# Transposes, casts and differences of a gated block over both token halves in one instruction

## The chip, the cores and the metric

The kernel runs on one core of a Trainium2 chip. The metric is the device time of one execution in microseconds; the time given for a kernel is the median of its runs. Engines are named as the profile does: PE is TensorE (PEld its weight loads), DVE is VectorE, ACT is ScalarE, POOL is GpSimd, SP is SyncE.

## The reference

One decoder block over 256 tokens of width 2048, in float32. A feed-forward block (FFN), a mixer, a second FFN and a gated embedding each add to `h`:

```python
def swiglu(x, w_gu, w_down):
    gate, up = jnp.split(x @ w_gu, 2, axis=-1)
    return (jax.nn.silu(gate) * up) @ w_down

h = h + 0.5 * swiglu(rms_norm(h, ffn1_norm[i]), ffn1_w_gu[i], ffn1_w_down[i])
h = h + hybrid_mixer(rms_norm(h, mix_norm[i]), w_in[i], ...)
h = h + 0.5 * swiglu(rms_norm(h, ffn2_norm[i]), ffn2_w_gu[i], ffn2_w_down[i])
gate = jax.nn.sigmoid(rms_norm(h, ple_norm[i]) @ ple_w_gate[i])
h = h + gate * (p[i] @ ple_w_proj[i])
```

The hidden width of an FFN is 5632. The change lies in the two FFNs alone, between `silu(gate) * up` and the product with `w_down`.

## The kernel before

**Products.** Every float32 operand of a large product is split into a rounded half `hi`, of type fp32r, and the remainder `lo`; a product is then three matmuls, hi by hi, hi by lo and lo by hi (lines L540, L541 and L542 in the FFNs). The stationary operand is a 128x128 piece of the activations, transposed (features on the partitions, tokens along the row), and the moving one is 128x512 of weights. The split of weights is done as they arrive: ACT casts (`whi`, L74) and DVE subtracts (`wlo`, L75), on tiles of 128x1024. Part of the FFNs' products goes by a scheme with seven products instead of eight on half matrices; it needs sums of weights (`R`, L304 and L311), which are split by L295 (ACT, `shi`) and L296 (DVE, `slo`), their matmuls are L334 to L336, and L341 and L342 add intermediate results.

**An FFN.** The hidden width is 11 blocks of 512, in three parts of 3, 4 and 4 blocks (`PARTS`). For each block the gate and up products of both token halves (t = 0 and 1, 128 tokens each) end in PSUM; after a part's blocks come that part's products with `w_down`, in two groups of 1024 output columns. The last block of a part is therefore needed soonest after it is made.

**The block of the change**, `down_input`, once per block, 22 times in the kernel. For both token halves: L477 multiplies up and silu(gate) into `sil` (128 tokens by 512 features per half). L482 transposes 32x32 squares of it on DVE into `tb`, one instruction per half. The squares are then brought into place by DMAs through DRAM: L487 writes `tb` to `scr`, L491 and L492 read it back into `tT`, in four pieces. L499 casts `tT` on ACT to `hTh`, the hi half, and L500 subtracts on DVE to `hTl`; again one instruction per token half. `hTh` and `hTl` are the stationary operands of the down products, 4 pieces of 128 features by 256 tokens per tile. The DMAs are issued on ACT's queue, and on SP's for the last block of a part.

**Order.** `down_input` is a generator that is advanced once per step of the weight stream, so its parts stand in the program between other work: after the transposes, and eight steps (for the last block of a part, two or three) before the casts. Two instructions that depend on one another wait by semaphores; each engine runs its own queue in order. A planner sets the order of each queue when the program is built, from its own estimate of when each instruction's inputs are ready, with the program's order as the priority. `keep` in the code, for all but the last block of a part, holds an instruction at its place in the program's order.

The same chain of transposes is also in `transposed` (L169) for the norms and the mixer, and a like split in `gate` (L1273); they stay as they are.

Of the kernel before, what the change touches and what calls it, by code (L numbers as in the profile page):

```python
# [13 lines left out]
ALU = mybir.AluOpType  # L14
AX = mybir.AxisListType

P = 128
# [26 lines left out]
def block_kernel(ctx, tc, a, out):  # L44
    nc = tc.nc
# [418 lines left out]
    def ffn(n, nT, r, scale, next_norm, stat):  # L464
        xs = picker(*nT)
        late = callable(r)
        with tc.tile_pool(name="ffn", bufs=1) as fp:
            hTh, hTl = [], []

            def down_input(u, sil, th, tl, last):  # L470

                queue, keep = (nc.sync, lambda x: x) if last else (nc.scalar, tc.keep_in_program_order)
                for t in range(2):
                    nc.vector.scalar_tensor_tensor(out=sil[:, t, :], in0=u[t], scalar=r[:, t:t + 1], in1=sil[:, t, :],  # L477
                                                   op0=ALU.mult, op1=ALU.mult)
                yield
                tb = fp.tile([P, 4, 2, P], F32, tag="tT", name="tb")  # L480
                for t in range(2):
                    nc.vector.transpose(tb[:, :, t].rearrange("p c (j x) -> p c j x", j=4),  # L482
                                        sil[:, t, :].rearrange("p (j c x) -> p c j x", j=4, c=4))
                if not last:
                    yield
                scr = dr.tile([P, 4, 2, P], F32, tag="scr2", name="scr2", bufs=2)
                keep(queue.dma_start(out=scr, in_=tb))  # L487
                for _ in range(2):
                    yield
                tT = fp.tile([P, 4, 2, P], F32, tag="tT", name="tT")  # L490
                for c in range(4):  # L491
                    keep(queue.dma_start(out=tT[32 * c:32 * c + 32].rearrange("x q t i -> x q (t i)"),  # L492
                                         in_=scr[:, c].rearrange("(q x) t i -> x q (t i)", q=4)))
                for _ in range(last or 8):
                    yield
                for t in range(2):
                    hi, lo = (x[:, :, t * P:(t + 1) * P].rearrange("p j (q y) -> p q j y", q=4) for x in (th, tl))
                    tv = tT[:, :, t].rearrange("p q (j y) -> p q j y", j=4)
                    keep(nc.scalar.copy(hi, tv))  # L499
                    keep(nc.vector.tensor_tensor(out=lo, in0=tv, in1=hi, op=ALU.subtract))  # L500

            def gated(g):
                sil = fp.tile([P, 2, NB], F32, tag="sil", name="sil")
                for t in range(2):
                    nc.scalar.activation(sil[:, t, :], g[t], AF.Silu, scale=r[:, t:t + 1])
                return sil
# [4 lines left out]
            for group, todo in ffn_plan[n]:  # L511
# [15 lines left out]
                for kind, one in todo:  # L527
# [5 lines left out]
                    for j in range(2):  # L533
# [3 lines left out]
                        for t in range(2):  # L537
                            c = slice(t * P, (t + 1) * P)
                            out = group.banks[2 * b + t]
# [19 lines left out]
                    elif b == 0:  # L559
                        if not late:  # L560
                            sil = gated(outs)
                    else:
                        if late:
                            r = r()
                            sil = gated(group.banks[0:2])
                            late = False
                        th = fp.tile([P, 4, T], F32R, tag="hTh", name="hTh", bufs=max(i1 - i0 for i0, i1 in PARTS))
                        tl = fp.tile([P, 4, T], F32R, tag="hTl", name="hTl", bufs=max(i1 - i0 for i0, i1 in PARTS))
                        hTh.append(th)
                        hTl.append(tl)  # L570
                        i0, i1 = PARTS[group.part]

                        last = (3 if i1 - i0 == 4 else 2) if len(hTh) == i1 else 0
                        gen = down_input(outs, sil, th, tl, last)
                        next(gen)

                        lanes.finish(0)
                        lanes.add(0, gen)
                        if last:
                            lanes.advance(0)  # L580
# [58 lines left out]
    with tc.tile_pool(name="fin", bufs=1) as fp:  # L639
# [35 lines left out]
        for _, (nb, g) in todo:  # L675
            whi, wlo = next_weights()
            for j in range(2):
                k = 2 * g + j
                xh, xl = xs(k)
                for t in range(2):  # L680
                    c = slice(t * P, (t + 1) * P)
# [17 lines left out]
        for t in range(2):  # L699
# [6 lines left out]
            for j in range(4):  # L706
                c = slice(j * NB, (j + 1) * NB)
# [670 lines left out]
```

## Time and profile before

| what | value |
|---|---|
| median of 3 runs | 1947.38 us (1946.30 to 1947.69) |
| span of the profiled execution, first to last instruction | 1944.1 us |
| median less that span | 3.3 us |
| PE busy / DVE busy / ACT busy | 1927.9 / 1603.2 / 1163.4 us |
| mean granted TensorE clock | 0.999 |
| L482 transposes | 44, 30.3 us in all |
| L499 casts | 44, 25.0 us in all |
| L500 differences | 44, 28.7 us in all |

The profile gives of the profiled execution its span, from the first to the last instruction; a time of its own beyond that isn't recorded. Busy shares are averages over stages. An instruction's duration and the time until the next one of its engine starts are two things, as the next can start before the first has ended.

### The profile page before, as it was taken

How to read it: one execution, taken by the hardware profiler on the slowest of the kernel's cores; microseconds unless marked ns; L12 is line 12 of the kernel's file. 1: busy time of each engine (PE TensorE's matmuls, PEld its weight loads, DVE VectorE, ACT ScalarE, POOL GpSimd, SP SyncE). 2: the span in 40 equal slices, each digit the busy share in tenths (PEclk: the TensorE clock that was granted, in tenths of full speed). 3: DMA queues.
4: the chain of work that ended last, by engine and by line, in shares of the span. 5: the costliest groups of instructions: out<-in, count | busy, mean ns of one | idle time of the engine just before them, and what ended most of it. 6: DMA issues, size and time to landing. Idle time of an engine off the chain costs nothing.

```text
span 1944.1 us, 24295 instructions
## 1 busy us (share of the span) xinstructions
PE 1927.9 (99%) x8882; PEld 1593.1 (82%) x8882; DVE 1603.2 (82%) x1743; ACT 1163.4 (60%) x1358; POOL 148.8 (8%) x226
## 2 busy tenths in 40 slices
PE   9999999999999999999999999999999999999998
PEld 7888888888888888878788888888888888888887
DVE  7879988998889866797856679899888998889965
ACT  6655656566665567654555456566565755657654
POOL 0010110000001000010100000011000100001000
PEclk9999999999999999999999999999999999999999
DMA  8778898898898765556464776788898988989864
GB/s 306 269 217 291 256 292 272 248 296 247 269 288 255 224 218 171 173 167 218 159 215 157 243 278 229 236 268 285 260 278 253 306 257 261 264 263 273 253 212 147
DMA packets 144183, 475.06 MB, mean 244 GB/s; under 512 B 19648, under 2 KB 47296, under 8 KB 129856
## 3 DMA queue, kind: packets, MB, share of 16 engines
q1 hardware_dynamic: 104896, 293.78, 43.6%
q0 software_dynamic: 25920, 160.44, 29.9%
q10 hardware_dynamic: 13248, 19.30, 3.3%
q8 instruction: 69, 1.13, 0.2%
q14 instruction: 50, 0.41, 0.1%
HBM read 451.44 MB, written 22.02 MB: 244 GB/s over the span
## 4 chain that ended last, share of the span: by engine, by line
PE 91%; DVE 6%; issue 1%; DMA 1%; ACT 1%; POOL 0%; SPq 0%; POOLq 0%; DVEq 0%; ACTq 0%
PE d L540 5%; PE d L541 5%; PE d L542 5%; PE u L541 5%; PE u L542 5%; PE u L540 5%; PE g L541 4%; PE g L542 4%; PE pj L109 4%; PE pj L110 4%; PE pj L111 4%; PE g L540 4%; PE g L335 4%; PE g L334 4%; PE g L336 4%; PE u L334 3%
## 5 line engine op out<-in xcount | busy, mean ns | idle before, releaser
L74 ACT CAST whi<-raw 128x1024 fp32r<-128x1024 f32 (+1 forms) x489 | 511.7, 1050 | 420.0 <-PE pj L111 108.9
L75 DVE TENSOR_TENSOR wlo<-raw,whi 128x1024 fp32r<-128x1024 f32 (+1 forms) x489 | 590.8, 1217 | 155.8 <-ACT whi L74 153.1
L296 DVE TENSOR_TENSOR slo<-R,shi 128x2048 fp32r<-128x2048 f32 (+2 forms) x224 | 444.4, 1987 | 99.9 <-ACT shi L295 99.7
L295 ACT CAST shi<-R 128x2048 fp32r<-128x2048 f32 (+2 forms) x224 | 374.0, 1673 | 185.6 <-DVE R L304 74.4
L109 PE MATMUL pj<-whi,nTh 128*128 128x512 f32 x448 | 179.4, 401 | 0.0
L110 PE MATMUL pj<-wlo,nTh 128*128 128x512 f32 x448 | 175.3, 391 | 1.4 <-DVE wlo L75 1.4
L111 PE MATMUL pj<-whi,nTl 128*128 128x512 f32 x448 | 174.9, 390 | 0.0
L541 PE MATMUL d<-wlo,hTh 128*128 128x512 f32 x448 | 174.4, 389 | 0.0
L542 PE MATMUL d<-whi,hTl 128*128 128x512 f32 x448 | 174.0, 389 | 0.0
L540 PE MATMUL d<-whi,hTh 128*128 128x512 f32 x448 | 173.1, 390 | 0.0
L541 PE MATMUL g<-wlo,nTh 128*128 128x512 f32 x400 | 156.1, 390 | 0.6 <-DVE wlo L75 0.6
L540 PE MATMUL g<-whi,nTh 128*128 128x512 f32 x400 | 154.9, 390 | 1.2 <-ACT whi L74 0.9
L542 PE MATMUL g<-whi,nTl 128*128 128x512 f32 x400 | 155.9, 390 | 0.0
L541 PE MATMUL u<-wlo,nTh 128*128 128x512 f32 x400 | 155.7, 389 | 0.1
L542 PE MATMUL u<-whi,nTl 128*128 128x512 f32 x400 | 155.6, 389 | 0.0
L540 PE MATMUL u<-whi,nTh 128*128 128x512 f32 x400 | 154.2, 389 | 0.0
L304 DVE TENSOR_TENSOR R<-R 128x2048 f32<-128x2048 f32 (+2 forms) x68 | 135.4, 1991 | 0.1
L110 PEld LDWEIGHTS pj<-wlo,nTh 128*128 128x128 f32 x448 | 84.2, 188 | 19.2 <-DVE wlo L75 3.0
L540 PEld LDWEIGHTS d<-whi,hTh 128*128 128x128 f32 x448 | 84.1, 188 | 17.9 <-ACT hTh L499 0.7
L542 PEld LDWEIGHTS d<-whi,hTl 128*128 128x128 f32 x448 | 84.1, 188 | 17.7
L111 PEld LDWEIGHTS pj<-whi,nTl 128*128 128x128 f32 x448 | 84.1, 188 | 17.5
L541 PEld LDWEIGHTS d<-wlo,hTh 128*128 128x128 f32 x448 | 84.1, 188 | 17.4
(327 smaller groups left out, 3482.5 us busy)
## 6 DMA issues: line engine op xcount, KB each, us to landing
raw<-in_w_gu SPq DMA_DIRECT2D x199, 512.0 KB, 5.7
raw<-in_w_down SPq DMA_DIRECT2D x112, 512.0 KB, 6.4
raw<-in_w_in SPq DMA_DIRECT2D x112, 512.0 KB, 3.4
R<-in_w_gu2q POOLq DMA_DIRECT2D x54, 1024.0 KB, 8.1
R<-in_w_gu1q POOLq DMA_DIRECT2D x48, 1024.0 KB, 8.7
raw<-in_w_out SPq DMA_DIRECT2D x32, 512.0 KB, 4.4
R<-in_w_down11q POOLq DMA_DIRECT2D x12, 768.0 KB, 6.8
R<-in_w_down12q POOLq DMA_DIRECT2D x12, 768.0 KB, 6.3
```

What stands on the lines that cost most here:

```text
L74: nc.scalar.copy(hi[:, j, :], raw[:, j, :])
L75: nc.vector.tensor_tensor(out=lo[:, j, :], in0=raw[:, j, :], in1=hi[:, j, :], op=ALU.subtract)
L109: nc.tensor.matmul(outs[t], xh[:, c], whi[:, j, :], start=st, stop=False)
L110: nc.tensor.matmul(outs[t], xh[:, c], wlo[:, j, :], start=False, stop=False)
L111: nc.tensor.matmul(outs[t], xl[:, c], whi[:, j, :], start=False, stop=sp)
L295: keep(nc.scalar.copy(hi, w))
L296: nc.vector.tensor_tensor(out=lo, in0=w, in1=hi, op=ALU.subtract)
L304: keep(nc.vector.tensor_tensor(out=self.raw[x], in0=self.raw[x], in1=self.raw[y], op=ALU.add))
L334: nc.tensor.matmul(out, xh, whi[:, g, :], start=st, stop=False, skip_group_check=True)
L540: nc.tensor.matmul(out, xh[:, c], whi[:, j, :], start=st, stop=False, skip_group_check=True)
L541: nc.tensor.matmul(out, xh[:, c], wlo[:, j, :], start=False, stop=False, skip_group_check=True)
L542: nc.tensor.matmul(out, xl[:, c], whi[:, j, :], start=False, stop=sp, skip_group_check=True)
```

## The change

In `down_input`, the loops over t around L482 and around L499 and L500 are gone. The transposes of both halves are one instruction on a view with one more dimension, and so are the cast and the difference. What is computed, the tiles and the DMAs stay. Each of the three kinds goes from 44 instructions of 128x512 to 22 of 128x1024; `hTh` and `hTl` are each written by one instruction for both token halves.

```diff
                 tb = fp.tile([P, 4, 2, P], F32, tag="tT", name="tb")
-                for t in range(2):
-                    nc.vector.transpose(tb[:, :, t].rearrange("p c (j x) -> p c j x", j=4),
-                                        sil[:, t, :].rearrange("p (j c x) -> p c j x", j=4, c=4))
+                nc.vector.transpose(tb.rearrange("p c t (j x) -> p c t j x", j=4),
+                                    sil.rearrange("p t (j c x) -> p c t j x", j=4, c=4))
                 if not last:
                     yield
...
                 for _ in range(last or 8):
                     yield
-                for t in range(2):
-                    hi, lo = (x[:, :, t * P:(t + 1) * P].rearrange("p j (q y) -> p q j y", q=4) for x in (th, tl))
-                    tv = tT[:, :, t].rearrange("p q (j y) -> p q j y", j=4)
-                    keep(nc.scalar.copy(hi, tv))
-                    keep(nc.vector.tensor_tensor(out=lo, in0=tv, in1=hi, op=ALU.subtract))
+                hi, lo = (x.rearrange("p j (t q y) -> p t q j y", t=2, q=4) for x in (th, tl))
+                tv = tT.rearrange("p q t (j y) -> p t q j y", j=4)
+                keep(nc.scalar.copy(hi, tv))
+                keep(nc.vector.tensor_tensor(out=lo, in0=tv, in1=hi, op=ALU.subtract))
```

## The prediction

> **What bounds the kernel now.** I read the page's busy times first, then who TensorE waited for, then three stretches of time, then the instructions around the changed lines.
>
> ```profile
> span 1944.1 us, 24295 instructions
> PE 1927.9 (99%) x8882; PEld 1593.1 (82%) x8882; DVE 1603.2 (82%) x1743; ACT 1163.4 (60%) x1358; POOL 148.8 (8%) x226
> PEclk9999999999999999999999999999999999999999
> PE 91%; DVE 6%; issue 1%; DMA 1%; ACT 1%; POOL 0%; SPq 0%; POOLq 0%; DVEq 0%; ACTq 0%
> ```
>
> TensorE is busy for 1927.9 of 1944.1 us at a full granted clock in every slice, and the chain that ended last lies on it for 91%. So 16.2 us are not matmul, and they include the start, the last writes and the matmuls' wait for the first weights. What TensorE's matmuls lost to other engines is this (who waited for whom; us in total, times, longest us):
>
> ```profile
> PE pj L110 <- DVE wlo L75: 1.4, 3, 0.6
> PE vp L1109 <- DVE R L1130: 1.2, 1, 1.2
> PE idle L130 <- DVE stat L229: 1.1, 1, 1.1
> PE g L540 <- ACT whi L74: 0.9, 1, 0.9
> PE at L1221 <- DVE st L1214: 0.7, 1, 0.7
> PE g L541 <- DVE wlo L75: 0.6, 2, 0.4
> PE d L335 <- DVE slo L296: 0.6, 2, 0.3
> PE u L335 <- DVE slo L296: 0.3, 1, 0.3
> PE g L540 <- ACT nTh L158: 0.3, 1, 0.3
> ```
>
> These nine rows add up to 7.1 us, 0.36% of the span. That is the ceiling of any gain from relieving DVE and ACT, and most of it (pj, vp, at, idle) stands in the mixer or at the start, which the change doesn't touch. The share of busy time of DVE, 82%, is an average; in some stretches DVE has no pause at all (columns: the stretch, its length, then busy time and instructions of PE, PEld, DVE, ACT and POOL):
>
> ```profile
> 51.00:67.00 16.00, 15.47 (x67) 12.04 (x65) 15.91 (x12) 8.33 (x9) 0.00 (x0) 1.00 0.94 370
> 145.70:161.00 15.30, 15.01 (x67) 12.10 (x65) 15.30 (x18) 8.15 (x9) 0.89 (x1) 1.00 0.86 251
> 1288.60:1304.00 15.40, 15.12 (x67) 12.20 (x67) 15.40 (x18) 8.25 (x9) 0.88 (x1) 1.00 0.84 254
> ```
>
> In the second and third stretch, the ends of the first part of either FFN, DVE is busy for 15.30 of 15.30 and 15.40 of 15.40 us. Each ends with one of the two waits of d L335 for slo L296, 0.3 us each. There the length of the DVE queue sets TensorE.
>
> **The change, part by part.** It touches 22 groups (44 instructions of each kind, two per group):
>
> ```profile
> L482 DVE STREAM_TRANSPOSE tb<-sil 128x512 f32<-128x512 f32 x44 | 30.3, 698 | 0.0
> L500 DVE TENSOR_TENSOR hTl<-tT,hTh 128x512 fp32r<-128x512 f32 x44 | 28.7, 683 | 0.5 <-ACT hTh L499 0.5
> L75 DVE TENSOR_TENSOR wlo<-raw,whi 128x1024 fp32r<-128x1024 f32 x487 | 589.4, 1219 | 153.0 <-ACT whi L74 150.2 <-DMA tT<-scr 1.5
> L296 DVE TENSOR_TENSOR slo<-R,shi 128x2048 fp32r<-128x2048 f32 x133 | 304.1, 2288 | 81.0 <-ACT shi L295 80.8
> L499 ACT CAST hTh<-tT 128x512 fp32r<-128x512 f32 x44 | 25.0, 618 | 2.9 <-DMA tT<-scr 2.8
> L74 ACT CAST whi<-raw 128x1024 fp32r<-128x1024 f32 x487 | 510.5, 1052 | 417.2 <-PE pj L111 108.9 <-PE d L542 91.3 <-PE g L542 56.2
> ```
>
> Removed are 22 instructions of each of the three kinds; the 22 left become twice as wide. A merged difference is like L75, 1219 ns; a merged cast like L74, 1052 ns. No 128x1024 transpose is in the trace; taking the difference's price plus the 15 ns by which the narrow forms differ (698 less 683) gives 1234 ns. Its bounds are 1219 ns (as cheap as a difference) and 1396 ns (twice 698, nothing saved); I take 1234, because the narrow transpose is so near the narrow difference.
>
> The sum of single durations overstates what an engine saves, because neighbours overlap. The rows of two in a row show it, and they stand in the two places of the first FFN that matter. Call place A the tail of part 0's last tile (163 us), and place B the tile before it (147 us):
>
> ```profile
> 162.38 1.05 ACT L295 CAST shi<-R 128x1024 fp32r<-128x1024 f32 x1 [1.12 <-PE d L336]
> 163.34 1.14 ACT L499 CAST hTh<-tT 128x512 fp32r<-128x512 f32 x2
> 163.98 1.29 DVE L500 TENSOR_TENSOR hTl<-tT,hTh 128x512 fp32r<-128x512 f32 x2 [0.24 <-ACT hTh L499]
> 164.00 0.19 PEld L540 LDWEIGHTS d<-whi,hTh 128*128 128x128 f32 x1 [0.33 <-ACT hTh L499]
> 164.79 0.19 PEld L542 LDWEIGHTS d<-whi,hTl 128*128 128x128 f32 x1
> 165.02 0.19 PEld L541 LDWEIGHTS d<-wlo,hTh 128*128 128x128 f32 x1
> ...
> 1306.94 0.19 PEld L540 LDWEIGHTS d<-whi,hTh 128*128 128x128 f32 x1 [0.33 <-ACT hTh L499]
> ```
>
> ```profile
> 147.04 1.28 DVE L500 TENSOR_TENSOR hTl<-tT,hTh 128x512 fp32r<-128x512 f32 x2
> 147.55 0.61 PE L540 MATMUL d<-whi,hTh 128*128 128x512 f32 x2
> 147.78 0.19 PEld L542 LDWEIGHTS d<-whi,hTl 128*128 128x128 f32 x1
> 148.00 0.19 PEld L540 LDWEIGHTS d<-whi,hTh 128*128 128x128 f32 x1
> 148.23 0.19 PEld L541 LDWEIGHTS d<-wlo,hTh 128*128 128x128 f32 x1
> 149.37 1.30 DVE L482 STREAM_TRANSPOSE tb<-sil 128x512 f32<-128x512 f32 x2
> ```
>
> Queue time: two differences take 1.28 us, one wide 1.22, so 0.06 is saved; two transposes take 1.30, one wide 1.23, so 0.07; two casts take 1.14, one wide 1.05, so 0.09. Over 22 groups that is 2.9 us of DVE and 2.0 us of ACT, nearly all of it under TensorE's matmuls, which cover it. Cover is gone only where DVE is full: the two stretches that end at 161 and 1304 us hold one pair of each kind, so DVE comes 0.13 us earlier, of the 0.3 us that TensorE waits there: -0.26 us for both. In the stretch 51 to 67 us, DVE is full as well (15.91 of 16.00), with one transposed group and no difference: -0.07 us. The earlier transposes also let their round trip through DRAM start 0.1 us sooner; that is worth nothing at place A, because the casts there are queued on ACT behind shi L295, which waited 1.12 us for TensorE.
>
> The Trainium skill gives two prices for the overhead of an instruction. Its page "VectorE: DVE Perf Modes" (section on the TRN2 errata) has a measured fixed term of about 150 cycles, an estimated 0.16 us, that a large tile pays once; "Perfetto Trace Analysis" (Optimizing Scalar/DVE Operations) has about 60 ns on DVE and 93 ns on ScalarE of engine-busy time. The pairs above, 0.06 and 0.09 us, agree with the second; by the first the two full stretches would give the whole wait, -0.6 us, and the sum below would be about +0.2.
>
> Now the cost. TensorE reads hTh and hTl as stationary operands, the first half of the tokens first. At place A it waits for the first half's cast (0.33 us already) and starts at 164.00, right when 163.34 plus 0.62 is over. The merged cast is over 1.05 us after its start instead of 0.62, so this start moves by 0.43 us. No other work stands ready: the matmul in front had itself waited for ACT. Both FFNs have the place (0.33 us in both rows): +0.86 us. The bounds are 0 (if other matmuls are put ahead) and the same plus a wait for hTl, taken next.
>
> hTl at place A: its first half is ready at 163.98 + 0.68 = 164.66 and loaded at 164.79. Merged, it starts when the cast ends, 164.41, and is ready at 165.63, so that load moves 0.84 us; 0.43 of it the cast has already cost, 0.41 us would be new. At place B the first half is ready at 147.72 and loaded at 147.78; merged it is ready at 148.26, 0.5 us late. But L540 and L541, which need only hTh, follow at once (165.02; 148.00 and 148.23) and can go ahead. The order in the trace already does that: two L540 in a row at 147.55, while the program's order is 540, 541, 542. The planner that orders the matmuls thus allows for a late hTl. I take 0 for both, with the upper bounds 0.41 and 0.5 us per FFN.
>
> The other 18 groups: TensorE's weight loads have one row behind these tiles,
>
> ```profile
> PEld d L540 <- ACT hTh L499: 0.7, 2, 0.3
> ```
>
> which is place A twice; none waits for hTl, and no matmul in the list above names either. Matmuls on other tiles cover the rest.
>
> Sum: +0.86 - 0.26 - 0.07 = +0.53 us on the profiled span of 1944.1. The median of the runs, 1947.38, is 3.28 us above that span, work around it that the change leaves alone; so the prediction is 1947.38 + 0.53 = **1947.9 us**.
>
> **The rivals.** *Kept order.* If the matmuls keep their order, A costs 0.41 us more per FFN. B's 0.5 us lets the full DVE stretch catch up: TensorE comes to its wait at 161 us 0.5 later, DVE 0.13 earlier, and 0.3 of wait is absorbed, so the net is +0.2 instead of -0.13. Sum: 2 x (0.43 + 0.41 + 0.2) - 0.07 = +2.0, or 1949.4. For it: loads come 0.06 and 0.13 us after their data. Against it: the pulled-ahead L540.
>
> *Grouping pays, waits vanish.* If the planner fills place A with other matmuls, only the gains stay: -0.33, or with the waits of d L335, u L335 and the longest of g L541 (0.6 + 0.3 + 0.4) gone, -1.3: 1946.1. Against it: nothing ready at A.
>
> *The wide instruction blocks the queue: slower.* In the three stretches where DVE is full, a merged transpose or difference put ahead of the slo or wlo that TensorE needs next costs up to its 1.22 us each, since DVE has no pause to make it good. Three of those are +3.7, with A's +0.86 +4.5: 1951.9. It decides from the third such place on; one or two stay at +3.3 or less. For it: between 51 and 67 us the two transposes of a group are not neighbours today, a wlo goes between them:
>
> ```profile
> 53.51 0.70 DVE L482 STREAM_TRANSPOSE tb<-sil 128x512 f32<-128x512 f32 x1
> 54.14 1.19 DVE L75 TENSOR_TENSOR wlo<-raw,whi 128x1024 fp32r<-128x1024 f32 x1
> ```
>
> Against it: slo of 2048 elements go through the same queue at 2288 ns each, 133 times, and TensorE waits for hardly any of them. "Perfetto Trace Analysis" in the Trainium skill, same section, has a rule on this side: where an unsaturated engine causes bubbles on others, splitting its instructions lets work finish sooner. By it the change is wrong at place A and right only in the three full stretches; it is my +0.86 against -0.33.
>
> *The change doesn't do what it says*: the strided wide forms cost as much as two narrow ones. Then the gains are 0 and A costs 0.62 instead of 0.43 us, +1.2: 1948.6, inside the range.
>
> **How the numbers follow.** Forecast 0.55, kept order 0.18, wide forms no cheaper 0.07, grouping pays 0.10, blocked queue 0.10. What a measurement tells from no change is 0.2%, 3.9 us. A gain of 3.9 needs over half of the 7.1 us of waits, most of which are out of reach: faster 0.03. Slower takes the blocked queue and a little of the kept order with a mishap: 0.11. Same: 0.86. The range reaches from the grouping case less the spread of the runs shown (1946.30 to 1947.69), 1945.2, to the blocked queue, 1952.0; the forecast's own is 1947.1 to 1949.4.
>
> **What would show it.** Right: 22 instructions each on the merged lines, 1.05, 1.22 and 1.23 us; at 163 and 1306 us the wait of d L540 for hTh goes from 0.33 to about 0.76 us; the wait of d L335 for slo falls from 0.3 to about 0.17. Wrong: a new wait for hTl (kept order), a wide transpose well over 1.3 us, or TensorE waits for wlo or slo of a microsecond each between 51 and 67, 146 and 161, 1289 and 1304 us.

## The result and the profile after

The kernel after the change takes 1953.29 us (median; 1952.58 to 1955.53), the kernel before, beside it, 1947.11 us (1945.95 to 1947.69). The ratio is 1.0035 with a 95% interval of 1.0024 to 1.0046: slower by 6.2 us. The forecast was 1947.9 and its range ended at 1952.0. The span of the profiled execution went from 1944.1 to 1951.9 us.

Below, DVE takes a wide transpose, L481; L486 stores `tb` to `scr`; L491 reads it back into `tT`; L497 casts and L498 subtracts. The FFN's matmuls are L538, L539 and L540. L295 to L336 and L460 keep their numbers. The page of the kernel after, its busy times and the shares of its chain:

```profile
span 1951.9 us, 24216 instructions
PE 1932.4 (99%) x8882; PEld 1593.4 (82%) x8882; DVE 1602.2 (82%) x1699; ACT 1162.3 (60%) x1336; POOL 148.4 (8%) x226
...
PE 88%; DVE 7%; issue 2%; ACT 1%; DMA 1%; POOL 0%; SPq 0%; DVEq 0%; POOLq 0%; ACTq 0%
```

TensorE's share of the chain that ended last fell from 91 to 88%.

The edit itself came out as priced (instructions | busy us, mean ns of one):

```profile
L481 DVE STREAM_TRANSPOSE tb<-sil 128x1024 f32<-128x1024 f32 x22 | 27.2, 1238 | 0.0
L498 DVE TENSOR_TENSOR hTl<-tT,hTh 128x1024 fp32r<-128x1024 f32 x22 | 26.8, 1216 | 0.0
L497 ACT CAST hTh<-tT 128x1024 fp32r<-128x1024 f32 x22 | 22.9, 1043 | 1.0 <-DMA tT<-scr 1.0
```

Yet a row that was not there before leads the list of what matmuls waited for (total, times, longest us):

```profile
PE d L334 <- ACT Sh L460: 3.0, 4, 1.3
...
PE d L538 <- ACT hTh L497: 0.9, 2, 0.4
```

Sh is a cast of a sum of token halves, of another kind of product (`d` from `shi` and `Sh`). The edit doesn't touch its line. Its four waits stand in the third block of the parts with four blocks, near 359, 608, 1506 and 1754 us; these are called the four places below. The first two of these stretches before, and then after (stretch, length, busy us and instructions of PE, PEld, DVE, ACT, POOL, then clock, DMA share, GB/s):

```profile
345.00:362.00 17.00, 17.00 (x76) 14.08 (x75) 16.31 (x21) 8.91 (x10) 1.71 (x2) 1.00 0.79 214
596.00:614.00 18.00, 18.00 (x81) 14.92 (x80) 15.88 (x21) 10.49 (x11) 1.37 (x2) 1.00 0.94 215
```

```profile
345.00:362.00 17.00, 16.17 (x71) 12.74 (x70) 15.41 (x17) 7.66 (x7) 1.76 (x2) 1.00 0.75 204
596.00:614.00 18.00, 16.59 (x72) 13.06 (x71) 14.27 (x19) 8.34 (x10) 0.88 (x1) 1.00 0.79 193
```

Before, TensorE runs 157 matmuls in these 35 us without a gap; after, 143. At 18.00 / 81 = 0.222 us each the 14 missing ones are 3.1 us. Taken more finely: both traces hold 8882 matmuls, and subtracting the start of the k-th before from that of the k-th after gives the lag at each point. It grows by 1.41, 2.02, 1.41 and 0.95 us in the four places, 5.8 in all, of 7.6 at the last matmul.

TensorE's own order moved as well. At each of the four places the first `d` L334 that needs Sh stands three matmuls earlier than before (near 357 us behind nine matmuls of `u` instead of twelve), some 0.7 us. Whether that order costs anything by itself is answered by the run with the small loads below, which keeps it.

What happens there is in the rows around 347 us. Before (start, length, engine, line, operation, idle time before it in brackets):

```profile
344.45 0.70 DVE L482 STREAM_TRANSPOSE tb<-sil 128x512 f32<-128x512 f32 x1
345.08 1.72 DVE L304 TENSOR_TENSOR R<-R 128x1536 f32<-128x1536 f32 x1
346.72 0.70 DVE L482 STREAM_TRANSPOSE tb<-sil 128x512 f32<-128x512 f32 x1
347.10 0.89 POOL L311 DMA_DIRECT2D R<-in_w_down11q  x1 [9.95 <-DVE R L304]
347.45 0.34 ACTq L487 DMA_DIRECT2D scr<-tb  x1
...
350.80 1.57 ACTq L492 DMA_DIRECT2D tT<-scr  x2
353.42 1.49 ACT L295 CAST shi<-R 128x1536 fp32r<-128x1536 f32 x1 [1.66 <-DVE R L304]
```

After:

```profile
344.89 1.75 DVE L304 TENSOR_TENSOR R<-R 128x1536 f32<-128x1536 f32 x1
346.56 1.24 DVE L481 STREAM_TRANSPOSE tb<-sil 128x1024 f32<-128x1024 f32 x1
346.94 0.89 POOL L311 DMA_DIRECT2D R<-in_w_down11q  x1 [9.21 <-DVE R L304]
347.83 0.34 ACTq L486 DMA_DIRECT2D scr<-tb  x1
351.96 1.75 DVE L304 TENSOR_TENSOR R<-R 128x1536 f32<-128x1536 f32 x1
356.32 0.31 ACTq L491 DMA_DIRECT2D tT<-scr  x1
356.73 1.48 ACT L295 CAST shi<-R 128x1536 fp32r<-128x1536 f32 x1 [3.92 <-DVE S L458]
358.11 1.04 ACT L460 CAST Sh<-S 128x1024 fp32r<-128x1024 f32 x1
359.20 0.50 PE L334 MATMUL d<-shi,Sh 128*128 128x512 f32 x1 [0.73 <-ACT Sh L460]
```

The DMAs that start between 347 and 349 us, before and then after (queue, KB each, us to landing):

```profile
R<-in_w_down11q POOLq DMA_DIRECT2D x1, 768.0 KB, 8.3
scr<-tb ACTq DMA_DIRECT2D x1, 512.0 KB, 3.3
```

```profile
R<-in_w_down11q POOLq DMA_DIRECT2D x1, 768.0 KB, 8.0
scr<-tb ACTq DMA_DIRECT2D x1, 512.0 KB, 8.5
```

Read it as a chain. Before, one half transpose stood ahead of the sum R (L304) and one behind it. The wide one goes behind R whole. R releases POOL's accumulating load (L311), the transpose releases the store. So the store now comes 0.89 us behind the load instead of 0.35, and lands after 8.5 us instead of 3.3. The read-back waits for it: 347.83 + 8.5 = 356.3, and the first of its four pieces is issued at 356.32. This issue and the casts shi and Sh are in ACT's queue, in this order, so the casts wait too. The profile names S L458 as what ended the 3.92 us, but shi reads R, which is done at 351.96 + 1.75 = 353.71; the row that ends just before shi is the read-back's issue. TensorE then waits for Sh.

### The profile page after: what moved, and what is told of

Same layout as the page of the kernel before. It is cut to its first block, busy times and chain, and to the rows that moved or that the text cites. A ratio compares the mean times of both kernels' runs of the same rounds, so it can differ in the third digit from the quotient of the medians.

```text
span 1951.9 us, 24216 instructions
## 1 busy us (share of the span) xinstructions
PE 1932.4 (99%) x8882; PEld 1593.4 (82%) x8882; DVE 1602.2 (82%) x1699; ACT 1162.3 (60%) x1336; POOL 148.4 (8%) x226
## 4 chain that ended last, share of the span: by engine, by line
PE 88%; DVE 7%; issue 2%; ACT 1%; DMA 1%; POOL 0%; SPq 0%; DVEq 0%; POOLq 0%; ACTq 0%
PE d L540 5%; PE d L539 5%; PE d L538 5%; PE u L539 4%; PE u L540 4%; PE u L538 4%; PE pj L109 4%; PE pj L110 4%; PE pj L111 4%; PE g L335 4%; PE g L336 3%; PE g L539 3%; PE g L334 3%; PE g L540 3%; PE g L538 3%; PE u L334 3%
## 5 line engine op out<-in xcount | busy, mean ns | idle before, releaser
L295 ACT CAST shi<-R 128x2048 fp32r<-128x2048 f32 (+2 forms) x224 | 373.5, 1672 | 197.5 <-DVE R L304 73.0
L538 PE MATMUL d<-whi,hTh 128*128 128x512 f32 x448 | 174.1, 390 | 0.9 <-ACT hTh L497 0.9
L539 PE MATMUL d<-wlo,hTh 128*128 128x512 f32 x448 | 174.4, 389 | 0.0
L540 PE MATMUL d<-whi,hTl 128*128 128x512 f32 x448 | 174.0, 390 | 0.3
L539 PE MATMUL g<-wlo,nTh 128*128 128x512 f32 x400 | 156.3, 391 | 0.5 <-DVE wlo L75 0.4
L540 PE MATMUL g<-whi,nTl 128*128 128x512 f32 x400 | 156.0, 390 | 0.0
L539 PE MATMUL u<-wlo,nTh 128*128 128x512 f32 x400 | 155.7, 389 | 0.2 <-DVE wlo L75 0.2
L538 PE MATMUL g<-whi,nTh 128*128 128x512 f32 x400 | 155.5, 391 | 0.3 <-ACT nTh L158 0.3
L540 PE MATMUL u<-whi,nTl 128*128 128x512 f32 x400 | 155.6, 389 | 0.0
L538 PE MATMUL u<-whi,nTh 128*128 128x512 f32 x400 | 155.0, 389 | 0.0
L304 DVE TENSOR_TENSOR R<-R 128x2048 f32<-128x2048 f32 (+2 forms) x68 | 135.7, 1996 | 0.1
L538 PEld LDWEIGHTS d<-whi,hTh 128*128 128x128 f32 x448 | 84.1, 188 | 19.0 <-ACT hTh L497 1.5
L540 PEld LDWEIGHTS d<-whi,hTl 128*128 128x128 f32 x448 | 83.9, 188 | 18.5 <-DVE hTl L498 1.1
L539 PEld LDWEIGHTS d<-wlo,hTh 128*128 128x128 f32 x448 | 84.1, 188 | 17.5
```

The source lines that it names most:

```text
L295: keep(nc.scalar.copy(hi, w))
L304: keep(nc.vector.tensor_tensor(out=self.raw[x], in0=self.raw[x], in1=self.raw[y], op=ALU.add))
L538: nc.tensor.matmul(out, xh[:, c], whi[:, j, :], start=st, stop=False, skip_group_check=True)
L539: nc.tensor.matmul(out, xh[:, c], wlo[:, j, :], start=False, stop=False, skip_group_check=True)
L540: nc.tensor.matmul(out, xl[:, c], whi[:, j, :], start=False, stop=sp, skip_group_check=True)
```

## The experiments

The theory: the late store costs most of the time, by way of ACT's queue. The rivals: the wide casts and differences (places A and B) cost it, or the wide transpose itself holds up what is behind it on DVE. All medians below are beside the kernel before on the same chip. The chips differ between groups of runs, and the kernel after alone took +6.2 us in one group and +8.2 in another (the row `again`), so a difference of 1 or 2 us between rows of different groups can't be read. The last column is steadier: it is how much TensorE's lag behind the kernel before, counted matmul by matmul as above, grows at the four places together in the profiled execution (over some 32 us around each).

| run | median us | before us | ratio and 95% interval | matmuls' wait of d for Sh (us, times) | lag gained at the four places (us) |
|---|---|---|---|---|---|
| the change | 1953.29 | 1947.11 | 1.0035 (1.0024 to 1.0046) | 3.0, 4 | 5.8 |
| e1_transposes | 1951.50 | 1946.09 | 1.0027 (1.0016 to 1.0038) | 4.1, 4 | 5.6 |
| e2_splits | 1946.69 | 1946.09 | 1.0005 (0.9996 to 1.0014) | none | 0.0 |
| e5_small_accum | 1948.16 | 1946.09 | 1.0011 (1.0002 to 1.0020) | none | 0.0 |
| e7_late_scr | 1959.79 | 1946.09 | 1.0067 (1.0054 to 1.0080) | 4.1, 4 | 10.5 |
| e3_readback_later | 1950.95 | 1945.71 | 1.0027 (1.0017 to 1.0036) | none | 3.6 |
| e6_last_halves | 1951.37 | 1945.71 | 1.0028 (1.0018 to 1.0038) | 2.4, 4 | 5.2 |
| e8_both | 1949.38 | 1945.71 | 1.0015 (1.0006 to 1.0024) | none | 3.7 |
| e9_load_later | 1962.20 | 1945.67 | 1.0083 (1.0069 to 1.0097) | 0.9, 1 | 3.2 |
| e10_load_later_halves | 1959.24 | 1945.67 | 1.0068 (1.0055 to 1.0081) | 1.0, 1 | 3.2 |
| again | 1953.83 | 1945.67 | 1.0039 (1.0027 to 1.0052) | 2.4, 4 | 5.3 |
| e11_ahead | 1949.03 | 1945.84 | 1.0018 (1.0008 to 1.0027) | none | 1.3 |

**Each part alone.** First (e1) the transposes alone are merged; casts and differences stay in halves.

```diff
+ nc.vector.transpose(tb.rearrange(...), sil.rearrange(...))
  for t in range(2):
      keep(nc.scalar.copy(hi, tv))
      keep(nc.vector.tensor_tensor(out=lo, in0=tv, in1=hi, op=ALU.subtract))
```

> The changed kernel with only the transposes merged; casts and differences stay two per block. Theory (the store of the transposed block to DRAM is issued after the accumulating weight load instead of just behind its start, lands about 5 us later, and the read-back that waits for it stands in front of casts in ACT's queue): the median time from issue to landing of the 16 stores on ACT's queue is 6 us or more (3.3 before, 7.8 after), d L334 waits for the cast Sh at four places, 2 to 3 us in all, and the time is 1951 to 1953 us. The wait for the cast hTh at places A stays at 0.33 us. Rival (the wide casts and differences are the cause): no wait of d L334 for Sh, and 1946.5 to 1947.5 us.

Then (e2) the casts and differences alone; the transposes stay in halves.

```diff
  for t in range(2):
      nc.vector.transpose(tb[:, :, t]..., sil[:, t, :]...)
+ keep(nc.scalar.copy(hi, tv))
+ keep(nc.vector.tensor_tensor(out=lo, in0=tv, in1=hi, op=ALU.subtract))
```

> The changed kernel with only the casts and differences merged; the transposes stay two per block. Theory: stores land as before (about 3.3 us median), no wait of d L334 for Sh, the wait for hTh at places A goes to 0.8 us each and hTl is waited for at places B: 1947.5 to 1949 us. Rival (wide casts and differences are the main cause): 1951 us or more.

The wide transposes alone cost 5.4 us, the wide casts and differences 0.6 (the second median is 0.8 us below its range, and the first run waits 4.1 us for Sh where 2 to 3 were expected). Transposes alone, the longest row of matmuls' waits (total, times, longest us), and then all such stores of the run (count, KB, median us to landing):

```profile
PE d L334 <- ACT Sh L460: 4.1, 4, 1.4
```

```profile
scr<-tb ACTq DMA_DIRECT2D x16, 512.0 KB, 7.8
```

The weight loads' waits with the casts and differences alone, where such a store takes 3.3 us as before:

```profile
PEld d L539 <- ACT hTh L498: 1.5, 2, 0.8
...
PEld d L541 <- DVE hTl L499: 1.1, 2, 0.6
```

The two costs add up to the whole (5.4 + 0.6 against 6.2) and leave each its own mark: the late store and the waits for Sh go with the transposes, the waits for hTh and hTl with the casts and differences. At the four places the lag grows by 5.6 us with the wide transposes and by nothing with the wide casts and differences. That removes the rival of places A and B as the main cost. (The median of the 16 stores holds more than the four places; the last section takes them apart.)

**The transpose on DVE, or the load it follows?** (e5) The kernel after, but each accumulating load moves a quarter of its columns, so the sums of weights are left incomplete. The order of the instructions on DVE, ACT, TensorE and SP is that of the change; so is the store's place behind the load's issue.

```diff
- nc.gpsimd.dma_start(out=self.raw[x], in_=self.quarters[y[1]][y[0]], accum_op=ALU.add)
+ nc.gpsimd.dma_start(out=self.raw[x][:, :, 0:P],
+                     in_=self.quarters[y[1]][y[0]][:, :, 0:P], accum_op=ALU.add)
```

> The changed kernel, every engine's order unchanged, but each accumulating weight load on POOL's queue moves only 128 of the 512 columns; the sums of weights are left incomplete, so that part of the computation is left out. Theory: the stores land in about 4 us or less (7.8 after), the waits of d L334 for Sh fall from 3.0 us to under 0.7 in all, and the time falls to 1947 to 1949.5 us. Rival (the changed order of the instructions is the cause, whatever the transfers do): the waits of d L334 stay near 3 us and the time near 1953.

The DMAs under way between 346 and 349 us (queue, KB each, us to landing):

```profile
scr<-tb ACTq DMA_DIRECT2D x1, 512.0 KB, 3.7
R<-in_w_down11q POOLq DMA_DIRECT2D x1, 192.0 KB, 5.0
```

With a quarter of the data ahead of it, a store 0.88 us behind the load (348.06 and 347.18) lands in 3.7 us instead of 8.5, no matmul waits for Sh, and 4.1 of the 6.2 us are gone. At the four places TensorE's lag doesn't grow at all, where the kernel after gained 5.8 us. The wait for hTh is as in the kernel after (0.9 us in two waits). DVE's order is the same, so a wide transpose in the way there isn't the cost; TensorE's order is the same too, so the three matmuls by which `d` moved forward cost nothing by themselves. The run lightens the DMA engines elsewhere too, and the kernel before with the same small loads wasn't run, so 4.1 us is no clean price; what is gone at the four places is.

**A late store without the change.** (e7) The kernel before, with a copy of one element of `tb` onto itself on ACT ahead of the store, so that it slips (not for the last block of a part).

```diff
+ if not last:
+     keep(nc.scalar.copy(tb[0:1, 0, 0, 0:1], tb[0:1, 0, 0, 0:1]))
  scr = dr.tile([P, 4, 2, P], F32, tag="scr2", name="scr2", bufs=2)
```

> The kernel before, with two transposes, casts and differences per block, and one added ACT copy of a single element of the transposed tile onto itself ahead of the store, in all but the last block of a part. The store then waits for ACT to finish the cast it is in and is issued up to about 1 us later. Theory: the stores that now slip behind the accumulating load land 4 us or more later, d L334 waits for Sh at up to four places, and the time is 1949.5 to 1953.5 us. Rival (a late store is harmless; the wide instructions are the cause): 16 copies of some 0.2 us on an engine that is not full, 1947 to 1948 us.

The instructions around 348 us, where the store then takes 8.1 us, and the matmuls' two longest rows of waits:

```profile
347.42 0.89 POOL L311 DMA_DIRECT2D R<-in_w_down11q  x1 [9.95 <-DVE R L304]
348.59 0.18 ACT L487 COPY tb<-tb 1x1 f32<-1x1 f32 x1
348.80 0.37 ACTq L489 DMA_DIRECT2D scr<-tb  x1
```

```profile
PE d L334 <- ACT Sh L460: 4.1, 4, 1.3
PE u L543 <- DVE wlo L75: 3.3, 4, 0.8
```

Five of the 16 stores slip, to 1.12 to 1.39 us behind a load, and land after 6.8 to 8.4 us. With narrow transposes the same four waits for Sh appear. So the late store is enough for them. The time is another matter: +13.7 us, more than expected. Of the 11.7 us by which the profiled execution is longer, 10.5 are gained at the same four places. The waits of `u` for wlo, which follow each of the four waits for Sh about 2 us later, are not in the kernel after. The copy itself waits for ACT's running cast and holds up the whi casts behind it (3.1 us in four waits); whether that is the whole of the excess wasn't tested.

**Free ACT's queue.** (e3) The kernel after, with the read-back written one step of the weight stream later (casts one less after it), so that it stands behind the cast shi in ACT's queue.

```diff
- for _ in range(2):
+ for _ in range(2 if last else 3):
      yield
...
- for _ in range(last or 8):
+ for _ in range(last or 7):
      yield
```

> The changed kernel with the read-back from DRAM traced one step later, and the casts one step less after it, in all but the last block of a part. The transposes still stand behind the weight sum, so the store is still issued after the accumulating load; but in ACT's queue the casts shi and Sh now stand ahead of the read-back. Theory (the late store hurts only because the read-back's wait blocks the casts behind it on ACT): the store's median landing stays at 6 us or more, the waits of d L334 for Sh fall from 3.0 us to under 0.7 in all, and the time is 1946.5 to 1949.5 us. Rival (the late data itself, or the accumulating load's transfer, holds up TensorE): the waits stay near 3 us and the time above 1951.

The waits of matmuls and weight loads, and all such stores:

```profile
PE d L335 <- DVE slo L296: 1.7, 4, 0.4
...
PEld d L334 <- ACT Sh L460: 1.2, 4, 0.3
```

```profile
scr<-tb ACTq DMA_DIRECT2D x16, 512.0 KB, 7.9
```

The store is as late as before, and no matmul waits for Sh: with the read-back out of the way, the casts run (shi starts at 352.69 us instead of 356.73). But the time only fell to +5.2 us, 1.5 us above what was expected. The planner answered the edit with another order of TensorE's sums, and four waits for slo, near 368, 616, 1514 and 1762 us, took over: the lag grows by 0.7 us at each of them, 2.9 of the 3.6 us in the table. The edit changed two things, so it shows that the queue is the way from the store to Sh, not what freeing it alone would be worth.

**Places A and B.** (e6) The kernel after, with the cast and difference of a part's last block in halves again.

```diff
+ if last:
+     for t in range(2):
+         keep(nc.scalar.copy(hi, tv))
+         keep(nc.vector.tensor_tensor(out=lo, in0=tv, in1=hi, op=ALU.subtract))
+ else:
      keep(nc.scalar.copy(hi, tv))
      keep(nc.vector.tensor_tensor(out=lo, in0=tv, in1=hi, op=ALU.subtract))
```

> The changed kernel with the cast and the difference of the last block of each part again in two halves, everything else merged. Theory: the wait for hTh at places A falls from 0.8 back to 0.33 us each and hTl isn't waited for there; the waits for Sh stay near 3 us: about 1 us less than the changed kernel, 1951 to 1953 us. Rival (the wide casts of the last blocks carry the loss): 1948 us or less.

The waits of matmuls and weight loads:

```profile
PE d L334 <- ACT Sh L460: 2.4, 4, 1.0
...
PEld d L545 <- ACT hTh L499: 0.7, 2, 0.3
```

The wait for hTh at place A is back at 0.3 us each; Sh stays, and so does +5.7 us; that this is half a us less than 6.2 can't be read across two chips. Both edits together (e8):

> The changed kernel with both: read-back one step later, and the last block's cast and difference in two halves. Theory: both losses are gone, 1946 to 1948.5 us, no measurable gain over the kernel before, since TensorE waited for little there. Rival (merging pays once nothing is blocked): below 1944 us.

+3.7 us; it misses its expectation by 1 us, and the waits of d L335 for slo (1.7 us, 4 times) are still there.

**The load behind the store.** (e9; e10 has the last block's halves as well, and `again` is the kernel after beside them) The kernel after, with a copy of one element of R on POOL ahead of each accumulating load, to hold the load back until the store is out.

```diff
+ one = self.raw[x][0:1, 0, 0:1]
+ nc.gpsimd.tensor_copy(one, one)
  nc.gpsimd.dma_start(out=self.raw[x], in_=self.quarters[y[1]][y[0]], accum_op=ALU.add)
```

> The changed kernel with a copy of one element of the weight sum onto itself on POOL ahead of each accumulating weight load; the order on DVE, ACT, PE and SP is unchanged. The load is issued later by the length of that copy. Theory (the store must be issued before the load's transfer begins): at the four places where the store came 0.66 to 0.89 us after the load's issue it now comes before it or within 0.4 us, lands in about 3.3 us, the waits of d L334 for Sh are gone (under 0.7 us), and the time falls by some 4 us, to 1.5 to 2.5 us above the kernel before. If the copy is shorter than 0.4 us, nothing changes. Rival (not the start of the load but its amount of data in flight holds the store up): the store lands as late, and the time stays 5 us or more above the kernel before.

> The same one-element copy, and the last block's cast and difference of each part in two halves. Theory: the losses at the store and at places A are both undone; 0 to 1.5 us above the kernel before. Rival (merging pays once nothing is blocked): 1 us or more below the kernel before.

> The changed kernel once more, on the chip of these two runs: 5 to 7 us above the kernel before, 3 us of waits of d L334 for Sh.

As a remedy both failed (+16.5 and +13.6 us): all loads come later, and ACT's shi waits for R (matmuls lose 3.8 us to it at two places), while the kernel after again took +8.2, where 5 to 7 were expected. But the copies took 0.2 to 2.6 us, so the lag of the store differs from place to place within one run. The issues at 350 us with the store's landing, and then those at 1749 us:

```profile
349.95 0.89 POOL L313 DMA_DIRECT2D R<-in_w_down11q  x1 [0.30 <-POOL R L312]
350.60 0.34 ACTq L488 DMA_DIRECT2D scr<-tb  x1
```

```profile
scr<-tb ACTq DMA_DIRECT2D x1, 512.0 KB, 7.8
```

```profile
1748.79 0.88 POOL L313 DMA_DIRECT2D R<-in_w_down22q  x1 [0.53 <-POOL R L312]
1749.21 0.34 ACTq L488 DMA_DIRECT2D scr<-tb  x1
```

```profile
scr<-tb ACTq DMA_DIRECT2D x1, 512.0 KB, 3.4
```

0.65 us behind the load's issue the store needs 7.8 us, 0.42 us behind it 3.4. The place isn't the reason: in the kernel after, the store at this last place is 0.66 us behind the load and takes 8.0 us. TensorE follows: its lag grows by 0.8, 1.6 and 0.8 us at the three places whose store is late, and by nothing at the fourth.

**The wide transpose ahead of R.** (e11) Halves for the last block as in e6, and the read-back two steps later; the planner then puts the wide transpose ahead of R at the four places.

```diff
- for _ in range(2):
+ for _ in range(2 if last else 4):
...
- for _ in range(last or 8):
+ for _ in range(last or 6):
```

> The changed kernel with the last block's cast and difference of each part in two halves and the read-back two steps later; with it the merged transposes stand ahead of the weight sum R in DVE's order at the four places, so the store is issued before the accumulating load. Theory: the store lands in 3 to 4 us there, no wait of d L334 for Sh, and 1945.5 to 1948 us, within 1.5 us of the kernel before. Rival (merging pays once nothing is blocked): 1 us or more below it.

The issues around 347 us and the store's landing:

```profile
346.68 0.89 POOL L311 DMA_DIRECT2D R<-in_w_down11q  x1 [10.82 <-DVE R L304]
347.06 0.34 ACTq L486 DMA_DIRECT2D scr<-tb  x1
```

```profile
scr<-tb ACTq DMA_DIRECT2D x1, 512.0 KB, 3.3
```

Here the transposes are wide and the stores early: 0.15 to 0.38 us behind the load at the four places, landing in 2.7 to 3.3, with no wait for Sh. The read-back moved too, and e3 had no such wait with a late store; it is the early landing that counts here. The width doesn't make the store late, the place behind R does. The run still takes 3.2 us more than the kernel before; its changed order brings waits elsewhere, among them those of `d` for hTl (0.9 us) and for slo (0.8 us), once each, near 1293 and 1288 us. It is a little above what was expected. No version here beat the kernel before.

## Why the prediction was wrong

**The parts that were priced came out.** Durations: 1238, 1216 and 1043 ns against 1234, 1219 and 1052. Place A: the cast's end moved TensorE by 0.43 us in each FFN, as the term said. These rows of the kernel after are the answer to its rows of before:

```profile
163.40 1.04 ACT L497 CAST hTh<-tT 128x1024 fp32r<-128x1024 f32 x1
164.50 0.19 PEld L538 LDWEIGHTS d<-whi,hTh 128*128 128x128 f32 x1 [0.76 <-ACT hTh L497]
```

The wait is 0.76 us, the number forecast. The Trainium skill says on its page "Perfetto Trace Analysis" (Optimizing Scalar/DVE Operations) that breaking up the instructions of a ScalarE or VectorE that isn't saturated, but causes bubbles on other engines, may let work finish sooner. The traces agree here: ACT is 60% busy, and with the halves of e6 the wait is 0.3 us again. No wait for hTl came at A. Place B and the full DVE stretch behind it came to the right sum by another way, which is luck:

```profile
148.45 0.30 PEld L540 LDWEIGHTS d<-whi,hTl 128*128 128x128 f32 x2 [0.57 <-DVE hTl L498]
```

B was priced at 0 and cost 0.31 us; the stretch was priced at -0.13 and gave -0.45, for the whole of the 0.3 us wait at 161 us is gone. That is the mechanism of the rival *kept order*: TensorE comes later, DVE earlier, and the wait between them closes. Net -0.14 against -0.13, in each FFN. With A, both FFNs have 2 x (0.43 + 0.31 - 0.45) = +0.58 us, against 0.86 - 0.26 = +0.60 forecast. The run with casts and differences alone fits: +0.6 us, though its interval (0.9996 to 1.0014) can't tell that from nothing.

**The step that failed** is one sentence: "The earlier transposes also let their round trip through DRAM start 0.1 us sooner; that is worth nothing at place A". It took the queue saving for the whole effect and looked at place A alone. At four of the 18 groups that the prediction then put under "Matmuls on other tiles cover the rest", the store starts further behind the load, 0.66 to 0.89 us instead of 0.13 to 0.36. The first half transpose could be done ahead of R and the second right after it; one instruction has one place in the order, and it is behind R. The store then comes 1.27 us (347.83 less 346.56) after the start of the transpose behind R, where it came 0.73 us after it (347.45 less 346.72), and so falls further behind a load that R releases. At nine of ACT's other eleven stores it went the other way, and the store comes sooner behind its load: near 267 us 2.4 us instead of 4.7, as the wide transpose stands there where the first half stood. What merging does to the order thus differs from group to group, and the 0.1 us of the prediction is the size of neither shift. The trace of before has both rows that show what this can cost, the load's issue on POOL and the read-back in ACT's queue ahead of shi and Sh; the prediction read neither queue there.

The rival *blocked queue* had the sign and nearly the size (1951.9) by luck: it was for DVE's queue, in the three full stretches; none of its waits came. The queue that blocked was ACT's, and what blocked it was a DMA's issue. *Change doesn't do what it says* and *grouping pays* fell with the durations and with place A.

The account of the 7.6 us of lag: 5.8 at the four places, 0.58 at A and B, 0.44 in two waits of `g` for slo near 237 and 1385 us, and the remaining 0.8 in steps that, after the first 8 us, are at most 0.3 up or down and whose causes are open. Of the medians' 6.2 us, the run with the small loads gives 4.1 back.

One bound of the prediction doesn't come out of the terms that it names: the grouping case less the spread of the runs is 1946.1 - 1.4 = 1944.7, not 1945.2. Nothing hangs on it.

**Still open.** Why e7, the copy with the late store, gains 10.5 us at the four places and not about 6. How much of the waits for Sh, beside a late store, is due to the three matmuls by which `d` moved forward in the kernel after. What e3, e8 and e11 still lose, beyond the waits that their lists show: each moved TensorE's order along with the edit, and no run held it fixed. Whether the kernel after, with its transpose pinned ahead of R and nothing else moved, would be on a level with the kernel before wasn't tried.

## What to carry to other kernels

Two half instructions are also two places in an engine's order. Before merging them, look at what stands between them, which DMA each side releases, and what the DMA's landing holds up; here the wide transposes cost 5.4 us, against gains of 0.33 us that the prediction priced for the whole change. Price a merged instruction as queue time, as was done at A and B, and then follow its output's DMA to the next wait in every queue where it is issued.

## What the runs showed of the hardware

A 512 KB store from ACT's queue is sharply sensitive to its lag behind POOL's accumulating load. Five of the 16 such stores (four in e11) are issued within 1.4 us of a load's issue: those of the four places, behind 768 KB loads, and one near 1265 us, behind 512 KB, which also slips in the kernel after, to 6.1 us, without a wait for Sh. Over all runs with full loads, such a store issued 0.12 to 0.42 us after the load's issue landed in 2.6 to 3.7 us, 2.5 to 7.3 us ahead of the load; issued 0.64 to 0.89 us after, in 5.9 to 9.1; 1.12 to 1.39 us after, in 6.8 to 8.4. No run has a lag between 0.42 and 0.64. The load's issue on POOL lasts 0.89 us, and the late stores landed 0.2 to 2.8 us after the load did. With a quarter of the load's data, in packets of 512 instead of 6144 bytes (e5), stores 0.78 to 0.89 us behind landed in 3.5 to 3.9 us, ahead of the load.

The DMA packets in the traces show where the late store stands. In the kernel before, the store's first packet starts 0.9 us after its issue, and 0.51 MB of its queue and nothing of the load's move between 347.45 and 350.00 us; the load's first packet starts at 350.02, 2.9 us after its issue. In the kernel after, the load's first packet starts at 348.54, 1.6 us after its issue. Up to 351.00 us 0.36 MB of the load moves and nothing of the store, whose first packet starts at 351.46, 3.6 us after its issue; from then on both move. So the one whose packets start first holds the other off, the load by 1.3 us before (2.9 less 1.6) and the store by 2.7 after (3.6 less 0.9). The Trainium skill, page "DMA: Bandwidth & Descriptors" (Issuing engines are not separate DMA queues), says that DMAs of different engines run on the same 16 DMA engines and interleave. This trace agrees for the time from 351.46 us on, and not for the 2.9 us before it. Why the second one has to wait so long, the traces don't show.

Most other stores are issued 2.1 to 8.3 us behind an accumulating load that is still under way, and every one of these landed 1.4 to 4.0 us after it. In the kernel after they are mostly issued sooner behind their load; they take longer from issue to landing, but hardly land further past the load (by 0.13 us at most): near 267 us 8.3 us instead of 6.1 from issue, and 1.5 us past the load instead of 2.0. Part of the rise of the median of all 16 stores, from 3.3 to 7.8 us, is of this kind, so that median is no measure of the four places.

A second thing: an instruction that only issues a DMA, waiting for another DMA, holds up the compute behind it in its engine's queue (ACT is idle for 3.92 us, 3.0 of them after shi's input was done at 353.71), and the profile puts the wait down to a compute instruction that had nothing to do with it.
